# One decoder layer on one core: wider matmuls in the up stage and the projections, a first norm from transposed x, re-placed mixers and a split tail

## The chip, the cores and the metric

One core of a Trainium2 chip runs the kernel. The metric is the time of one launch in device microseconds: the median of three runs, and beside it one execution under the hardware profiler, whose trace is read here. TensorE is PE in the profile (PEld is its weight loads), VectorE is DVE, ScalarE is ACT, GpSimd is POOL, and SyncE (SP) issues most of the transfers. Each engine works through its own list in order.

## The reference

One layer, 256 tokens, 1024 channels, all in fp32. Three mixers share one projection: pooling over windows of 2 to 16, an mLSTM with 4 heads in two chunks of 128 tokens, and causal attention with 8 heads of 64 (one block of 256 keys, so plain causal softmax here).

```python
h = rmsnorm(x, ln1_g[l])
z = h @ w_in[l]                      # 1024 -> pool | mq mk | mv | mo | mi mf | aq ak av
...
mix = jnp.concatenate([po, hm, ao], axis=-1)
x = x + mix @ w_out[l]               # 1024 -> 1024
h2 = rmsnorm(x, ln2_g[l])
u = causal_dwconv(h2 @ w_up[l], ffn_conv[l])          # 1024 -> 2*2816, 3 taps
x = x + (jax.nn.silu(u[..., :D_FF]) * u[..., D_FF:]) @ w_down[l]   # 2816 -> 1024
```

## The kernel before, in words

All weights are read once, as 48 units of about 1 MB (`raw`, four buffers): 11 for the projection (`IN_UNITS`: of, vi, pool, mq, mk, and akA to avB for the two groups A and B of attention heads), 4 for W_out, 22 for W_up (a unit is a pair of 128 gate and 128 value columns), 11 for W_down. Each fp32 product is made of three matmuls in fp32r, a rounded fp32: a unit is split into `hi`, rounded on ACT (`split_hi`), and `lo` = raw − hi on DVE (`split_lo`), and so is the activation (`h_hi`, `h_lo`, later `mix_hi`, `a_hi` and so on); the matmuls are hi·hi, hi·lo and lo·hi, summed in PSUM. The last `split_lo` of a unit issues the load of the unit four further.

The stages follow one another: `of` and `vi` (gates, values), the other projections with the mixers between them, W_out with the residual (`xs` holds x by rows), the second norm, the first two up pairs by rows (`up_rows`, tile `upr`, transposed afterwards), the 20 other up pairs by columns (weights stationary, 256 tokens streaming), then the down stage into four PSUM blocks `acc[t, c]` (two halves of tokens, two of columns).

In the up stage PE works on pair i while ACT and DVE finish pair i−1: the last tap is a scaled copy on ACT (`fy`), the two others are DVE operations on `fy` that read PSUM, then silu on ACT, a product on DVE, and the split into `a_hi` (ACT) and `a_lo` (DVE). Between these lie the two halves of the next unit's split.

Everything ahead of the first up pair is cut into pieces, entered by `put(key, function, what it needs)`, and issued in the order of the numbers in the table `PLACE`; a piece without one has its number from `at`. `need` sets what a projection piece waits for. The order in the table is thus the order on every engine.

Names that come back below: `pg`, the transposes of the gates on PE, which need the evictions of of and vi and so the first norm's factors (`n1r`); `far` and `mb`, which carry a running maximum of the gates to DRAM and back to all partitions; `mqT` and `mkT`, the four-tap convolution of mLSTM's q and k (three DVE operations a tile, after `mqz`, `mkz`); `aqAsq`, squares of a projected query that ACT reads from PSUM.

Of the kernel before, what the change touches and what calls it, by code (L numbers as in the profile page):

```python
# [118 lines left out]
def kernel(  # L119
# [55 lines left out]
    def split_lo(u, part, parts):  # L175
        if u not in lo_t:
            lo_t[u] = wpool.tile([P, UMAX], F32R, tag="lo", name=f"lo{u}", bufs=HL_BUFS)
        n = unit_cols(u)
# [1 line left out]
        nc.vector.tensor_sub(lo_t[u][:, s], raw_t[u][:, s], hi_t[u][:, s].bitcast(F32))  # L180
# [24 lines left out]
    def load_part(u, c, parts):  # L205
        n = UMAX // parts
        nc.sync.dma_start(raw_t[u][:, c * n:(c + 1) * n], wg[u][:, c * n:(c + 1) * n])

    for q in range(4):
        c = slice(KT * (q > 0) + 2 * S * q, KT + 2 * S * (q + 1))  # L210
# [1 line left out]
        load_part(0, q, 4)
    for t in range(NT):
        load_part(1, t, 2)
        nc.sync.dma_start(xs[:, t], x[t * P:(t + 1) * P])
# [1005 lines left out]
```

## The time and the profile before

| what | value |
|---|---|
| median of three runs | 314.95 us (314.52 to 315.57) |
| the profiled execution | 314.13 us |
| its span, first to last instruction | 312.4 us |
| granted clock of TensorE, mean | 0.998 |
| busy: PE, DVE, ACT, POOL | 299.7, 227.3, 184.7, 11.9 us |
| read from HBM | 53.86 MB |
| up stage | 132.4 to 247.7 us |
| down stage's matmuls | 247.7 to 308.6 us |

Busy shares are averages over the stages; what a stage is worth is read from the engine that bounds it there. A row of waits names the waiting engine, its tile and line, what ended the wait, the sum, the number of times and the longest. A row of the chain gives start, length and what ran. A row of groups gives line, engine, operation, output and inputs with their shapes, the count, then busy time, mean ns of one, and the idle time ahead of them.

### The profile page before, as it was taken

Reading aid. Unit: us, or ns where it says so; the run is one execution under the profiler, and the core shown is the slowest. Engines: PE = TensorE matmul, PEld = TensorE weight load, DVE = VectorE, ACT = ScalarE, POOL = GpSimd, SP = SyncE. Lnnn points to the kernel's source line nnn. Section 1 sums busy time; section 2 is a strip of 40 time slices with the busy share of each in tenths; the row PEclk is TensorE's granted clock in tenths of the full one; section 3 lists DMA queues with packets and bytes.
Section 4 is the critical chain, followed back from the end, with each engine's and each line's share of the span. In section 5 each row is a group of like instructions: output and inputs, shape, how many; then the busy total and the mean of one; then the engine's idle time right before and its main releaser. Section 6 shows DMA issues by size and latency. Waiting matters only on the chain.

```text
span 312.4 us, 5418 instructions
## 1 busy us (share of the span) xinstructions
PE 299.7 (96%) x2132; PEld 274.4 (88%) x2132; DVE 227.3 (73%) x444; ACT 184.7 (59%) x359; POOL 11.9 (4%) x30
## 2 busy tenths in 40 slices
PE   7987969899999999999999999999999999999995
PEld 3877969899987789999999999999999988888883
DVE  2756899999869667689988788788788786534111
ACT  3884659977878526858566475565664594324000
POOL 1004540000000000000000000000000000000000
PEclk9999999999999999999999999999999999999999
DMA  7997616333514760151564463554644649600003
GB/s 232 426 410 325 221 66 259 134 136 134 212 60 137 269 266 2 56 217 58 214 237 168 150 250 141 193 213 137 212 193 148 231 159 403 270 2 0 0 12 125
DMA packets 9545, 55.26 MB, mean 177 GB/s; under 512 B 1060, under 2 KB 1328, under 8 KB 3632
## 3 DMA queue, kind: packets, MB, share of 16 engines
q1 hardware_dynamic: 9216, 53.99, 46.7%
q10 hardware_dynamic: 304, 0.92, 0.8%
q8 instruction: 17, 0.28, 0.4%
q14 instruction: 8, 0.07, 0.1%
HBM read 53.86 MB, written 1.05 MB: 176 GB/s over the span
## 4 chain that ended last, share of the span: by engine, by line
PE 80%; DMA 7%; ACT 6%; DVE 5%; issue 1%; SPq 0%; ACTq 0%; DVEq 0%
PE dn L818 19%; PE up L306 12%; PE up L304 12%; PE up L305 12%; PE wo L818 7%; DMA xs<-in_x 2%; ACT hi L173 2%; DVE lo L180 2%; DMA raw<-in_wg 2%; DMA raw<-in_w 2%; PE upr L313 1%; DVE mqT L470 1%; PE upr L315 1%; PE upr L314 1%; DMA far<-mr 1%; PE akB L313 1%
## 5 line engine op out<-in xcount | busy, mean ns | idle before, releaser
L180 DVE TENSOR_TENSOR lo<-raw,hi 128x1024 fp32r<-128x1024 f32 (+2 forms) x102 | 116.1, 1160 | 25.6 <-ACT hi L173 25.5
L173 ACT ACTIVATE hi<-raw 128x1024 fp32r<-128x1024 f32 (+2 forms) x102 | 98.2, 992 | 27.5 <-PE dn L818 18.6
L304 PE MATMUL up<-h_hi,hi 128*128 128x256 f32 x320 | 90.3, 282 | 0.0
L306 PE MATMUL up<-h_hi,lo 128*128 128x256 f32 x320 | 90.2, 282 | 0.0
L305 PE MATMUL up<-h_lo,hi 128*128 128x256 f32 x320 | 90.1, 281 | 0.0
L304 PEld LDWEIGHTS up<-h_hi,hi 128*128 128x128 f32 x320 | 60.7, 190 | 0.0
L306 PEld LDWEIGHTS up<-h_hi,lo 128*128 128x128 f32 x320 | 60.6, 189 | 0.0
L305 PEld LDWEIGHTS up<-h_lo,hi 128*128 128x128 f32 x320 | 60.6, 189 | 0.0
L1075 DVE SCALAR_TENSOR_TENSOR fy<-up,par,fy 128x255 f32<-128x255 f32 x88 | 41.8, 480 | 15.1 <-ACT fy L1072 13.5
L1072 ACT ACTIVATE fy<-up,par 128x256 f32<-128x256 f32 x44 | 20.1, 466 | 32.0 <-PE up L306 32.0
L818 PE MATMUL dn<-hi,a_lo 128*128 128x512 f32 x88 | 28.1, 393 | 0.0
L818 PE MATMUL dn<-lo,a_hi 128*128 128x512 f32 x88 | 28.1, 393 | 0.0
L818 PE MATMUL dn<-hi,a_hi 128*128 128x512 f32 x88 | 28.1, 392 | 0.0
L818 PEld LDWEIGHTS dn<-hi,a_lo 128*128 128x128 f32 x88 | 16.5, 188 | 3.8
L818 PEld LDWEIGHTS dn<-lo,a_hi 128*128 128x128 f32 x88 | 16.5, 188 | 3.8
L818 PEld LDWEIGHTS dn<-hi,a_hi 128*128 128x128 f32 x88 | 16.4, 188 | 3.7
L231 ACT ACTIVATE a_hi<-fy 128x256 fp32r<-128x256 f32 x22 | 9.2, 418 | 11.8 <-DVE fy L1081 11.8
L1123 DVE TENSOR_TENSOR xs<-dn,xs 128x512 f32<-128x512 f32 (+1 forms) x5 | 2.7, 579 | 16.7 <-PE dn L818 16.7
L818 PE MATMUL wo<-hi,mix_hi 128*128 128x512 f32 x32 | 11.2, 412 | 0.0
L818 PE MATMUL wo<-lo,mix_hi 128*128 128x512 f32 x32 | 10.6, 393 | 0.0
L818 PE MATMUL wo<-hi,mix_lo 128*128 128x512 f32 x32 | 10.6, 392 | 0.0
L1080 ACT ACTIVATE fy<-fy 128x256 f32<-128x256 f32 x22 | 9.0, 408 | 2.2 <-DVE fy L1075 2.2
(286 smaller groups left out, 521.3 us busy)
## 6 DMA issues: line engine op xcount, KB each, us to landing
raw<-in_w SPq DMA_DIRECT2D x46, 1024.0 KB, 4.8
raw<-in_wg SPq DMA_DIRECT2D x4, 260.0 KB, 5.3
raw<-in_wg SPq DMA_DIRECT2D x2, 520.0 KB, 6.8
xs<-in_x SPq DMA_DIRECT2D x2, 512.0 KB, 7.8
x_t<-in_xt SPq DMA_DIRECT2D x3, 256.0 KB, 5.1
mb<-far ACTq DMA_DIRECT2D x1, 768.0 KB, 3.8
out_y<-xs SPq DMA_DIRECT2D x3, 256.0 KB, 2.0
par<-in_params SPq DMA_DIRECT2D x1, 337.0 KB, 9.8
```

The lines of the kernel that those rows point to most:

```text
L173: nc.scalar.activation(hi_t[u][:, s], raw_t[u][:, s], AF.Copy)
L180: nc.vector.tensor_sub(lo_t[u][:, s], raw_t[u][:, s], hi_t[u][:, s].bitcast(F32))
L231: nc.scalar.activation(hi, src, AF.Copy)
L304: nc.tensor.matmul(dst, a, h_hi[:, k, :], start=k == 0, stop=False)
L305: nc.tensor.matmul(dst, a, h_lo[:, k, :], start=False, stop=False)
L306: nc.tensor.matmul(dst, b, h_hi[:, k, :], start=False, stop=k == KT - 1)
L313: nc.tensor.matmul(dst, h_hi[:, k, ts_], hw[:, k, :], start=k == 0, stop=False)
L314: nc.tensor.matmul(dst, h_hi[:, k, ts_], lw[:, k, :], start=False, stop=False)
L818: nc.tensor.matmul(acc[t, c], a, b[:, k, o:o + n], start=st and i == 0, stop=sp and i == 2)
L1072: nc.scalar.activation(y, ps[j], AF.Copy, scale=pcol(c0 + 4 * NPAIR))
L1075: nc.vector.scalar_tensor_tensor(y[:, d:], ps[j][:, :S - d], pcol(c0 + 2 * NPAIR * tap), y[:, d:], op0=ALU.mult, op1=ALU.add)
L1080: nc.scalar.activation(y_t[i, 0], y_t[i, 0], AF.Silu)
```

## The change

Six things change together.

1. Up pairs 2 to 21: `h_hi` and `h_lo` become halves of one tile `h_2`, and w_hi multiplies both in one matmul of 512 columns; w_lo multiplies h_hi alone, 256. A unit is 16 matmuls of 512 and 16 of 256, where it was 48 of 256. The two halves of the result are added afterwards: a copy `zl` on ACT, an add `z` on DVE, both of 512 columns; the taps read `z` in SBUF and alternate between the two tiles. PSUM for it is a new pool of two two-bank tiles, in the place of the mixers' one.
2. The attention's projections are made in pairs (key and query of a group, both values): a unit holds half the rows for both, and a matmul has 512 columns (144 of them for 288). The first two up pairs do the same (48 for 96). The units' order is now of, vi, mq, mk, A0, A1, pool, B0, B1, V0, V1.
3. The first norm's sums are taken from the transposed x: four squares on ACT, three adds on DVE, four one-column matmuls (`n1s`). `xs` is loaded after unit 3 instead of ahead of unit 2. All eight row blocks of `of` are plain fp32 matmuls (16, where 8 were, with 24 in fp32r).
4. The transfers of `far` and `mb` are issued by SP instead of ACT.
5. `PLACE` is new throughout, and the second norm's pieces are cut finer (three transposes to a PSUM bank).
6. The last output block (token half 1, column half 1) is added to `xs` after unit 8; the rest of it runs as 12 matmuls of 384 and 12 of 128 columns with their own adds and transfers.

```diff
-    "rbt": 7.327, "rb": 9.568, ("of", 0): 6.2, ("of", 1): 6.6, ("vi", 0): 7.109, ("vi", 1): 7.926, "setup":
...
+    ("f", 0): 2.300, ("of", 0, 0): 2.350, ("of", 1, 0): 2.400, ("f", 1): 2.450, ("sq", 0): 2.500, ("h", 0): 2.550,
...
-IN_UNITS = ["of", "vi", "pool", "mq", "mk", "akA", "aqA", "akB", "aqB", "avA", "avB"]
+IN_UNITS = ["of", "vi", "mq", "mk", "A0", "A1", "pool", "B0", "B1", "V0", "V1"]
+PAIRS = {"A": ("akA", "aqA"), "B": ("akB", "aqB"), "V": ("avA", "avB")}
...
+    h_2 = cpool.tile([P, KT, 2, S], F32R, name="h_2")
+    h_hi, h_lo = h_2[:, :, 0, :], h_2[:, :, 1, :]
...
+    def next_loads():
+        load(RAW_BUFS - 1)
+        for t in range(NT):
+            nc.sync.dma_start(xs[:, t], x[t * P:(t + 1) * P])
+        load(RAW_BUFS)
...
+    def first_square(p):
+        ks = slice(*PARTS[p])
+        nc.scalar.activation(sqk[:, ks, :], xk[:, ks, :], AF.Square)
+
+    def first_sums_t():
+        ps = aux([P, NT], "n1s")
+        for t in range(NT):
+            for k in range(2):
+                nc.tensor.matmul(ps[:, t:t + 1], sqk[:, k, t * P:(t + 1) * P], ones[:, :1], start=k == 0,
+                                 stop=k == 1)
...
+        for k in (2 * half, 2 * half + 1):
+            kk = k if first else k + 4
+            nc.tensor.matmul(dst, h_hi[:, kk, ts_], hw[:, k, :], start=kk == 0, stop=False)
+            nc.tensor.matmul(dst, h_hi[:, kk, ts_], lw[:, k, :], start=False, stop=False)
+            nc.tensor.matmul(dst, h_lo[:, kk, ts_], hw[:, k, :], start=False, stop=kk == KT - 1)
...
-        nc.scalar.dma_start(sb["far"].rearrange("b h c -> h b c"), sb["mr"].rearrange("h (b c) -> h b c", c=P))
+        nc.sync.dma_start(sb["far"].rearrange("b h c -> h b c"), sb["mr"].rearrange("h (b c) -> h b c", c=P))
...
-        nc.scalar.dma_start(mb, sb["far"].partition_broadcast(P))
+        nc.sync.dma_start(mb, sb["far"].partition_broadcast(P))
...
+            for k in range(KT):
+                a, b = (w[:, k, j * P:j * P + P] for w in (hw, lw))
+                nc.tensor.matmul(ps[:, j], a, h_2[:, k].rearrange("p c t -> p (c t)"), start=k == 0, stop=False)
+                nc.tensor.matmul(ps[:, j, :S], b, h_hi[:, k, :], start=False, stop=k == KT - 1)
+
+    def up_sum(i):
+        ps = up_t[i]
+        zl = big(f"zl{i}")[:, :2 * S].rearrange("p (j t) -> p j t", t=S)
+        nc.scalar.activation(zl, ps[:, :, S:], AF.Copy)
+        z = big(f"z{i}")[:, :2 * S].rearrange("p (j t) -> p j t", t=S)
+        nc.vector.tensor_add(z, ps[:, :, :S], zl)
+        up_t[i] = [z[:, j, :] for j in range(2)]
...
+    finish(1, 1, queue=None)
...
+    for h, (sub, queue) in enumerate((((0, 384), nc.scalar), ((384, 512), nc.sync))):
+        acc[1, 1] = psum_u.tile([P, 2, 2 * S], F32, tag="up", name=f"tail{h}", bufs=2)[:, 0]
+        for i in last:
+            down(i, 1, (1,), last, sub)
+        finish(1, 1, sub, queue)
```

The re-placing shows best on DVE, where the first unit of attention is split. Before, unit 5 (akA; `lo5` is its second half here) on DVE:

```order
L457 TENSOR_TENSOR mqz1_496<-mq1_425,rb_114 128x256
L470 SCALAR_TENSOR_TENSOR mqT0_444<-mqz0_441,par_77,mqT0_444 128x255
L470 SCALAR_TENSOR_TENSOR mqT0_444<-mqz0_441,par_77,mqT0_444 128x254
L470 SCALAR_TENSOR_TENSOR mqT0_444<-mqz0_441,par_77,mqT0_444 128x253
L470 SCALAR_TENSOR_TENSOR mqT1_513<-mqz1_496,par_77,mqT1_513 128x255
L470 SCALAR_TENSOR_TENSOR mqT1_513<-mqz1_496,par_77,mqT1_513 128x254
L470 SCALAR_TENSOR_TENSOR mqT1_513<-mqz1_496,par_77,mqT1_513 128x253
L457 TENSOR_TENSOR mkz0_535<-mk0_482,rb_114 128x256
L180 TENSOR_TENSOR lo5_423<-raw5_211,hi5_421 128x1024
L180 TENSOR_TENSOR lo6_480<-raw6_286,hi6_478 128x1024
```

After the change the same place on DVE, where the first attention unit is unit 4 (A0) and the second unit 5 (A1):

```order
L503 TENSOR_TENSOR mqz0_375<-mq0_270,rb_114 128x256
L190 TENSOR_TENSOR lo4_377<-raw4_181,hi4_373 128x1024
L661 COPY cols_125<-mcols_391 128x2x4
L190 TENSOR_TENSOR lo5_414<-raw5_208,hi5_369 128x1024
L190 TENSOR_TENSOR lo4_377<-raw4_181,hi4_373 128x1024
L516 SCALAR_TENSOR_TENSOR mqT0_429<-mqz0_375,par_80,mqT0_429 128x255
L516 SCALAR_TENSOR_TENSOR mqT0_429<-mqz0_375,par_80,mqT0_429 128x254
L516 SCALAR_TENSOR_TENSOR mqT0_429<-mqz0_375,par_80,mqT0_429 128x253
L190 TENSOR_TENSOR lo6_453<-raw6_266,hi6_412 128x1024
L190 TENSOR_TENSOR lo5_414<-raw5_208,hi5_369 128x1024
```

The six taps and mkz stood between akA's split and what came ahead; now both halves of A0's split stand ahead of the first tap, and three taps ahead of the end of A1's. On PE, `pg` followed directly on vi and n1r; it now stands 12 matmuls of mq behind vi.

The gates' maximum before, on ACT (`hi3` is the unit of mq, `hi4` of mk):

```order
L597 DMA far_348<-mr_327 4x3x128
L600 DMA mb_118<-far_348 128x1536
L173 ACTIVATE hi3_333<-raw3_170 128x1024
L173 ACTIVATE hi4_390<-raw4_172 128x1024 x2
L173 ACTIVATE hi5_421<-raw5_211 128x1024 x2
```

And after the change on SP, among the loads (`raw7` is B0, `raw8` B1, `raw10` V1):

```order
L176 DMA raw6_266<-in_w 128x2048
L643 DMA far_334<-mr_328 4x3x128
L176 DMA raw7_350<-in_w 128x2048
L646 DMA mb_119<-far_334 128x1536
L176 DMA raw8_448<-in_w 128x2048
L176 DMA raw10_455<-in_w 128x2048
```

Both transfers left ACT, where splits stood behind them, for SP, where one load stands between them and the others behind.

One unit of the up stage on DVE, before (pair 11; `lo28` is the split of the unit that PE needs next):

```order
L1075 SCALAR_TENSOR_TENSOR fy110_2451<-up110_2331,par_77,fy110_2451 128x255
L1075 SCALAR_TENSOR_TENSOR fy110_2451<-up110_2331,par_77,fy110_2451 128x254
L1075 SCALAR_TENSOR_TENSOR fy111_2455<-up111_2332,par_77,fy111_2455 128x255
L1075 SCALAR_TENSOR_TENSOR fy111_2455<-up111_2332,par_77,fy111_2455 128x254
L180 TENSOR_TENSOR lo28_2461<-raw28_2187,hi28_2459 128x1024
L1081 TENSOR_TENSOR fy111_2455<-fy110_2451,fy111_2455 128x256
L180 TENSOR_TENSOR lo28_2461<-raw28_2187,hi28_2459 128x1024
L232 TENSOR_TENSOR a_lo_1684<-fy111_2455,a_hi_1683 128x256
```

and the same pair on DVE after the change:

```order
L1143 TENSOR_TENSOR z11_2092<-up11_2000,zl11_2090 128x512
L190 TENSOR_TENSOR lo28_2053<-raw28_1874,hi28_2037 128x1024
L1156 SCALAR_TENSOR_TENSOR fy110_2096<-z11_2092,par_80,fy110_2096 128x255
L1156 SCALAR_TENSOR_TENSOR fy111_2098<-z11_2092,par_80,fy111_2098 128x255
L1156 SCALAR_TENSOR_TENSOR fy110_2096<-z11_2092,par_80,fy110_2096 128x254
L1156 SCALAR_TENSOR_TENSOR fy111_2098<-z11_2092,par_80,fy111_2098 128x254
L1162 TENSOR_TENSOR fy111_2098<-fy110_2096,fy111_2098 128x256
L190 TENSOR_TENSOR lo29_2110<-raw29_1931,hi29_2094 128x1024
L239 TENSOR_TENSOR a_lo_1466<-fy111_2098,a_hi_1465 128x256
```

The add `z` is new at the unit's start, the taps alternate between the two tiles, and the halves of the split have moved half a unit ahead: the first half of unit 29 stands where the second of unit 28 stood.

More of the change, by code (lines that the diff above doesn't have):

```diff
@@ L29 @@
 WARM = 8
-FULL = (0, 1)
+PARTS = ((0, 2), (2, 4), (4, 6), (6, 8))
+FULL = range(4)
 HL_BUFS = 4
@@ L137 @@
     mix = ExitStack()
+    psum_m = mix.enter_context(tc.tile_pool(name="psum_m", bufs=4, space=bass.MemoryType.PSUM))
     mpool = mix.enter_context(tc.tile_pool(name="mpool", bufs=1))
@@ L203, with load_part @@
     raw_t[1] = wpool.tile([P, UMAX], F32, tag="raw", name="raw1", bufs=RAW_BUFS)
[L205 to L210, printed above, removed]
+    def load_part(u, a, b):
+        c = slice(a * UMAX // KT, b * UMAX // KT)
+        nc.sync.dma_start(raw_t[u][:, c], wg[u][:, c])
+    for a, b in PARTS:
+        c = slice(KT * (a > 0) + S * a, KT + S * b)
         nc.sync.dma_start(x_t[:, c], xt[:, c])
[L212 to L215, printed above, removed]
+        load_part(0, a, b)
+    for a in (0, 4):
+        load_part(1, a, a + 4)
     load(2)
@@ L333, with first_full, first_hi @@
     h_f = h_fb[:, :KT * S].rearrange("p (k c) -> p k c", c=S)
-    sq1 = wpool.tile([P, UMAX], F32, tag="lo", name="sq1", bufs=HL_BUFS)
+    sq1 = wpool.tile([P, UMAX], F32, tag="lo", name="sq1", bufs=HL_BUFS)[:, :KT * S]
+    sqk = sq1.rearrange("p (k c) -> p k c", c=S)
     rb = cpool.tile([P, S], F32, name="rb")
-    def pair(q):
-        return slice(2 * q, 2 * q + 2)
-    def first_full(q):
-        for k in (2 * q, 2 * q + 1):
+    def first_full(p):
+        for k in range(*PARTS[p]):
             nc.vector.tensor_scalar(h_f[:, k, :], xk[:, k, :], g1[:, k:k + 1], None, op0=ALU.mult)
-    def first_hi(q):
-        if q in FULL:
-            nc.scalar.activation(h_hi[:, pair(q), :], h_f[:, pair(q), :], AF.Copy)
+    def first_hi(p):
+        ks = slice(*PARTS[p])
+        if p in FULL:
+            nc.scalar.activation(h_hi[:, ks, :], h_f[:, ks, :], AF.Copy)
@@ L347, in first_hi, with first_lo @@
         else:
-            for k in (2 * q, 2 * q + 1):
+            for k in range(*PARTS[p]):
                 nc.scalar.activation(h_hi[:, k, :], xk[:, k, :], AF.Copy, scale=g1[:, k:k + 1])
-    def first_lo(q):
-        if q in FULL:
-            nc.vector.tensor_sub(h_lo[:, pair(q), :], h_f[:, pair(q), :], h_hi[:, pair(q), :].bitcast(F32))
+    def first_lo(p):
+        ks = slice(*PARTS[p])
+        if p in FULL:
+            nc.vector.tensor_sub(h_lo[:, ks, :], h_f[:, ks, :], h_hi[:, ks, :].bitcast(F32))
@@ L354, in first_lo @@
         else:
-            for k in (2 * q, 2 * q + 1):
+            for k in range(*PARTS[p]):
                 nc.vector.scalar_tensor_tensor(h_lo[:, k, :], xk[:, k, :], g1[:, k:k + 1],
                                                h_hi[:, k, :].bitcast(F32), op0=ALU.mult, op1=ALU.subtract)
-    n1v = []
-    def first_sum(t):
-        if not n1v:
-            n1v.append(tpool.tile([P, NT], F32, tag="n1v", name="n1v"))
-        nc.vector.tensor_scalar(n1v[0][:, t:t + 1], sst[t], 1.0 / D, EPS, op0=ALU.mult, op1=ALU.add)
+    def next_loads():
[3 more added lines that the diff above has]
+        load(RAW_BUFS)
@@ L366, in first_factors, with first_mean @@
+    def first_mean():
+        nc.vector.tensor_scalar(n1v, r_t["s"], 1.0 / D, EPS, op0=ALU.mult, op1=ALU.add)
     def first_factors():
@@ L424, in bulk_rows, with bulk_pair @@
         product_rows(u, ps_t[name, t], t, range(4 * half, 4 * half + 4))
+    def bulk_pair(name, t, half):
+        u, first = U[name], name[1] == "0"
+        if first and half == 0:
+            pr = mm([P, 512], f"{name[0]}{t}")
+            for c, n in enumerate(PAIRS[name[0]]):
+                ps_t[n, t] = pr[:, 256 * c:256 * c + 256]
+            ps_t[name[0], t] = pr
+        dst, ts_ = ps_t[name[0], t], slice(t * P, (t + 1) * P)
+        hw, lw = (d[u][:, :2048].rearrange("p (k c) -> p k c", c=512) for d in (hi_t, lo_t))
+        for k in (2 * half, 2 * half + 1):
[3 more added lines that the diff above has]
+            nc.tensor.matmul(dst, h_lo[:, kk, ts_], hw[:, k, :], start=False, stop=kk == KT - 1)
     def bulk_cols(name, j, half):
@@ L816, in rows_product @@
                 for c in cs:
-                    o, n = chunks[c]
-                    nc.tensor.matmul(acc[t, c], a, b[:, k, o:o + n], start=st and i == 0, stop=sp and i == 2)
+                    o, n = 512 * c + sub[0], sub[1] - sub[0]
+                    nc.tensor.matmul(acc[t, c][:, :n], a, b[:, k, o:o + n], start=st and i == 0, stop=sp and i == 2)
     def w_out(i, t, k, cs=(0, 1)):
@@ L849 @@
         put(("lo", 1, q), do(split_lo, 1, q, 4), ("hi", 1, q), at=(0.5, 1, 4.45, 4.55)[q])
-    for t in range(NT):
-        put(("n2", t), do(norm_square, t, 0, 1, "n1", sq1[:, t * D:(t + 1) * D]), at=(4.3, 4.6)[t])
-        put(("sum", t), do(first_sum, t), ("n2", t), at=4.65)
+    for p in range(NP):
+        put(("sq", p), do(first_square, p), at=2 * p - 8.45)
+    put("ld", next_loads, ("of", 1, NP - 1), *((n, p) for n in ("h", "l", "sq") for p in range(NP)), at=0.5)
+    for n in range(3):
+        put(("sa", n), do(first_add, n), *((("sq", 2 * n), ("sq", 2 * n + 1)) if n < 2 else (("sa", 0), ("sa", 1))),
+            at=(-5.5, -1.2, -1)[n])
+    put("n1s", first_sums_t, ("sa", 2), at=4.55)
+    put("sum", first_mean, "n1s", at=4.65)
     n = 4
-    done = {}
+    done, part = {}, {}
     for name in IN_UNITS[1:]:
-        f = bulk_rows if name[:2] in ("vi", "av", "aq", "ak") else bulk_cols
+        two = name[0] in PAIRS
+        f = bulk_pair if two else bulk_rows if name == "vi" else bulk_cols
         order = [(0, 0), (0, 1), (1, 0), (1, 1)]
-        for j, half in sorted(order, key=lambda o: o[::-1]) if name == "vi" else order:
+        for j, half in sorted(order, key=lambda o: o[::-1]) if two or name == "vi" else order:
             put(("b", n), do(f, name, j, half), at=n)
-            done[name, j] = ("b", n)
+            for m in PAIRS[name[0]] if two else (name,):
+                done[m, j] = ("b", n)
+            part[n] = (n // 4, half)
             n += 1
@@ L924 @@
     for t in range(NT):
-        put(("mN", t), do(mnum_t, t), *(("me", h) for h in range(4)), ("vi", 0), ("vi", 1))
+        put(("mN", t), do(mnum_t, t), *(("me", h) for h in range(4)), ("vi", 0), ("vi", 1), "setup")
         put(("md", t), do(mnum, t), ("mN", t), "gce")
@@ L987 @@
         if n < 8:
-            half = n // 6
-            need(("b", n), ("lo", 1, 1 + 2 * half), ("l", 1 + 2 * half))
+            half = part[n][1]
+            need(("b", n), *(("lo", 1, q) for q in range(2 * half, 2 * half + 2)),
+                 *(("l", p) for p in range(NP) if PARTS[p][0] < 4 * half + 4))
         elif n < 44:
-            need(("b", n), ("lo", n // 4, n % 2), ("l", 3))
+            need(("b", n), ("lo", *part[n]))
         elif n < 56:
@@ L1110 @@
-    split(U_DOWN + 1, 1)
-    def down(i, t, cs=(0, 1)):
+        for m in (0, 1) if i == 2 else (i - 1,):
+            if m > 1:
+                up_sum(m)
+            if i < NPAIR and m:
+                split_hi(u + 2, 0, 2)
+            up_last(m)
+            if i < NPAIR and m:
+                split_hi(u + 2, 1, 2)
+            if m > 1:
+                split_lo(u + 1, 1, 2)
+            up_taps(m)
+            up_gate(m)
+            if i < NPAIR and m:
+                split_lo(u + 2, 0, 2)
+            up_out(m)
@@ L1113, in down @@
+    def down(i, t, cs=(0, 1), span=(0, N_DOWN - 1), sub=(0, 512)):
         if i == 0:
             for c in cs:
-                acc[t, c] = (mm if t == 1 and c else aux)([P, 512], f"dn{t}{c}")
-        rows_product(U_DOWN + i, (a_hi, a_lo), 2 * i, i == 0, i == N_DOWN - 1, t, cs)
-    def finish(t, c, parts=1):
-        n = 512 // parts
-        for i in range(parts):
-            s = slice(c * 512 + i * n, c * 512 + i * n + n)
-            nc.vector.tensor_add(xs[:, t, s], acc[t, c][:, i * n:i * n + n], xs[:, t, s])
-            (nc.scalar if i else nc.sync).dma_start(out[t * P:(t + 1) * P, s], xs[:, t, s])
@@ L1126, with finish @@
-    for i in range(N_DOWN - 2):
-        for t in range(NT):
-            down(i, t)
-            split(U_DOWN + i + 2, t)
-    last = (N_DOWN - 2, N_DOWN - 1)
+                acc[t, c] = aux([P, 512], f"dn{t}{c}")
+        rows_product(U_DOWN + i, (a_hi, a_lo), 2 * i, i == span[0], i == span[1], t, cs, sub=sub)
+    def finish(t, c, sub=(0, 512), queue=nc.sync):
+        s = slice(c * 512 + sub[0], c * 512 + sub[1])
+        nc.vector.tensor_add(xs[:, t, s], acc[t, c][:, :sub[1] - sub[0]], xs[:, t, s])
+        if queue is not None:
+            queue.dma_start(out[t * P:(t + 1) * P, s], xs[:, t, s])
@@ L1131 @@
+    last = (N_DOWN - 2, N_DOWN - 1)
+    for i in range(last[0]):
+        down(i, 0)
+        split(U_DOWN + i + 2, 0)
+        down(i, 1, (0,))
+        down(i, 1, (1,), (0, last[0] - 1))
+        split(U_DOWN + i + 2, 1)
+    finish(1, 1, queue=None)
     for i in last:
@@ L1134 @@
         finish(0, c)
-    for c in range(2):
+    for i in last:
+        down(i, 1, (0,))
+    finish(1, 0)
+    for h, (sub, queue) in enumerate((((0, 384), nc.scalar), ((384, 512), nc.sync))):
+        acc[1, 1] = psum_u.tile([P, 2, 2 * S], F32, tag="up", name=f"tail{h}", bufs=2)[:, 0]
         for i in last:
-            down(i, 1, (c,))
-        finish(1, c, 1 + c)
+            down(i, 1, (1,), last, sub)
+        finish(1, 1, sub, queue)
 def _units(w_in, w_out, w_up, w_down):
```

190 lines of the change are left out of this document (99 added, 91 removed), and 97 rows, old and new, of the table PLACE.

## The prediction

> **What bounds the kernel now.** I read the page first (busy shares, the slices, the chain by engine), then busy time by stage, then what TensorE (PE) waited for, then the chain in order of time.
>
> ```profile
> PE 299.7 (96%) x2132; PEld 274.4 (88%) x2132; DVE 227.3 (73%) x444; ACT 184.7 (59%) x359; POOL 11.9 (4%) x30
> ...
> PE   7987969899999999999999999999999999999995
> ...
> PE 80%; DMA 7%; ACT 6%; DVE 5%; issue 1%; SPq 0%; ACTq 0%; DVEq 0%
> ```
>
> PE is busy 96% of the span and is 80% of the chain; its idle tenths lie in the first eight slices. By stage (projections' first part, mixers and W_out, up, down; the columns are the stretch, its length, then PE, PEld, DVE, ACT, POOL):
>
> ```profile
> 8.00:64.00 56.00, 49.05 (x402) 46.32 (x400) 45.39 (x89) 42.34 (x82) 10.37 (x19) 1.00 0.66 255
> 64.00:132.40 68.40, 68.39 (x485) 60.58 (x482) 52.54 (x153) 48.23 (x125) 0.00 (x0) 1.00 0.39 143
> 132.40:247.70 115.30, 115.30 (x970) 115.14 (x969) 99.51 (x170) 70.60 (x127) 0.00 (x0) 1.00 0.50 182
> 247.70:308.60 60.90, 60.87 (x264) 49.19 (x263) 27.04 (x27) 20.85 (x23) 0.00 (x0) 1.00 0.35 132
> ```
>
> So from 64 us on PE never waits, and only cheaper matmuls help there. PE's clock is full throughout (1.00). The 56 us before hold 6.95 us of PE idle, and PE's waits name it:
>
> ```profile
> PE akA L314 <- DVE lo L180: 2.4, 1, 2.4
> PE pg L571 <- ACT gates L451: 1.4, 2, 1.1
> PE mq L306 <- DVE lo L180: 1.2, 1, 1.2
> ...
> PE akB L313 <- ACT aqAsq L509: 0.8, 1, 0.8
> PE mq L304 <- ACT hi L173: 0.7, 1, 0.7
> PE of L314 <- DVE lo L180: 0.3, 1, 0.3
> ```
>
> They sum to 6.8 us. A wait costs a little more than its row, as a restart shows:
>
> ```profile
> 42.77 0.28 PE L313 MATMUL akA<-hi,h_hi 128*128 128x256 f32 x1
> 45.44 0.39 PE L314 MATMUL akA<-lo,h_hi 128*128 128x256 f32 x1 [2.39 <-DVE lo L180]
> ```
>
> Start to start this is 2.67 us, and a step is 0.12, so the wait cost 2.55, 0.16 over its row. Seven stalls (pg has two) are thus worth 6.8 + 7×0.16 = 7.9 us.
>
> **The change, part by part.** Widths first. The steps come from the chain and the stage above:
>
> ```profile
> 117.31 0.88 PE n2pt L283 x8
> ...
> 132.46 1.02 PE up L1028 x8
> 247.68 60.91 PE dn L818 x264
> 308.61 0.42 DVE xs L1123
> ```
>
> The up stage's 960 matmuls of 256 columns take 115.30 − 1.02 = 114.28 us, 0.119 each; a 512-wide one takes 60.91/264 = 0.231. Two merged into one save 0.238 − 0.231 = 0.0074 us. The up stage has 16×20 = 320 such merges: **−2.4 us**. Projections (144) and the first two up pairs (48): **−1.4 us**. [...]
>
> The "of" unit and the first sums are dearer:
>
> ```profile
> L439 PE MATMUL of<-raw,h_f 128*128 128x260 f32 x16 | 4.0, 392 | 1.1 <-DVE h_f L342 1.1
> ...
> L378 PE MATMUL n1r<-diag,ones 128*128 128x128 f32 x4 | 0.6, 274 | 0.0
> ```
>
> The 16 records are 8 plain fp32 matmuls, 0.5 us each. Eight more cost 4.0 and replace 24×0.12 = 2.9: **+1.1**. The four new one-column sums (n1s) have no row; the two n1r matmuls cost 0.3 each, so four lie between 0 and 1.2; a single column streams less than 128, so I take **+0.4**. The squares and adds that replace the xs squares run on ACT and DVE while PE is in "of", before anyone needs them.
>
> Now the stalls, **−7.9**. The rows that make them:
>
> ```profile
> 7.09 7.78 DMA xs<-in_x
> ...
> 25.03 3.21 DMA far<-mr
> 28.26 0.36 ACTq L600
> 28.67 1.06 ACT hi L173
> 29.75 1.71 DVE lo L180
> ```
>
> ```profile
> 39.70 4.22 DVE L470 SCALAR_TENSOR_TENSOR mqT<-mqz,par,mqT 128x255 f32<-128x255 f32 x6
> 43.83 0.42 DVE L457 TENSOR_TENSOR mkz<-mk,rb 128x256 f32<-128x256 f32 x1
> 44.17 2.35 DVE L180 TENSOR_TENSOR lo<-raw,hi 128x1024 fp32r<-128x1024 f32 x2
> ```
>
> ```profile
> 8.00:24.00 16.00, 14.18 (x110) 12.97 (x109) 11.18 (x23) 14.17 (x31) 0.00 (x0) 1.00 1.03 418
> ```
>
> - akA: six taps and mkz (4.6 us) stand ahead of the split that PE wants. Now both halves of A0's lo stand ahead of the taps.
> - mq, both rows: ACT held the issue of mb (L600) until far landed, and the splits behind it were late. On SP it holds no split. Price: on SP the load of B0 stands between the two, that of B1 behind mb. A far of 3.2 us can delay only those two, whose matmuls come after A0, A1 and pool (5.7 us a unit); I cost it at nothing, at 3.2 if that cover is gone.
> - pg: 12 matmuls of mq (1.4 us) now lie between vi and pg, and the norm no longer waits for xs, which landed at 14.87. Without its 1.05 MB ahead, at 418 GB/s, the later weights land 2.5 us earlier.
> - akB: needs the banks that aqAsq still reads; the pool unit (48×0.119 = 5.7 us) now stands between. of: no split is left to wait for.
>
> What is late next? DVE: its 97.9 busy us (45.39 + 52.54) out of 124.4 become as many out of some 116, 79% to 84%. I give back a quarter, **+2.0** (ends 0 and 7.9): nearer to none, because each stall's cause is moved by name; not none, because some 200 other pieces move too.
>
> Up stage, beside PE. PE's unit becomes 16×(0.231 + 0.119) = 5.60 us, from 5.71. DVE gains the add z, ACT the copy zl:
>
> ```profile
> L180 DVE TENSOR_TENSOR lo<-raw,hi 128x1024 fp32r<-128x1024 f32 x38 | 46.4, 1220 | 0.0
> L1075 DVE SCALAR_TENSOR_TENSOR fy<-up,par,fy 128x254 f32<-128x254 f32 x43 | 20.7, 482 | 1.5
> L1075 DVE SCALAR_TENSOR_TENSOR fy<-up,par,fy 128x255 f32<-128x255 f32 x43 | 20.6, 478 | 12.7 <-ACT fy L1072 12.7
> L1081 DVE TENSOR_TENSOR fy<-fy,fy 128x256 f32<-128x256 f32 x21 | 8.8, 418 | 0.2
> L232 DVE TENSOR_TENSOR a_lo<-fy,a_hi 128x256 fp32r<-128x256 f32 x21 | 8.8, 418 | 1.0 <-ACT a_hi L231 1.0
> ...
> L828 DVE TENSOR_TENSOR xs<-wo,xs 128x512 f32<-128x512 f32 x4 | 2.6, 683 | 1.4 <-PE wo L818 1.4
> ```
>
> These five up rows sum to 105.3 us in 114 of wall clock, yet the stage shows 99.51 busy in 115.3: neighbours overlap by some 0.04 us. Per unit (115.3/5.71 = 20.2) that is 4.93 us; z adds 0.683 − 0.04: 5.57 against 5.60. That is tight. But DVE may lag: z must be read only before the unit after next takes its PSUM pair, 5.60 after its last matmul, and zl and z take some 2×0.68, so 4.2 us of lag are free. 0.2 us per unit over 20 units would still cost nothing. I take **0**. ACT has 70.60/20.2 + 0.7 = 4.2 of 5.6.
>
> Tail: 12 of 264 matmuls become 12 of 384 (between 0.119 and 0.231, so 0.175) and 12 of 128 (0.88/8 = 0.11): 12×(0.285 − 0.231) = +0.65, between 0 (columns alone count) and +1.4 (384 as dear as 512, 128 as 256). The last add shrinks from two of 256 to one of 128, and its issue no longer waits for the second: the 0.42 us row goes, −0.4 (0 to −0.4). **+0.2**.
>
> Sum: −2.4 − 1.4 + 1.1 + 0.4 − 7.9 + 2.0 + 0.2 = −8.0. The profiled execution took 314.1 us (312.4 of span, 1.7 around it), so 306.1; it lies 0.8 under the median of 314.95, so I forecast a median of **306.9**.
>
> **Rivals.** (1) The stalls come back under other names, more than half: a DVE in 45.39 of 56 us already, hi and lo re-placed among 200 pieces, two loads behind the maximum's transfers. All 7.9 back instead of 2.0 gives 312.8; half to all, 308.9 to 312.8. Against: each of the five stalls has its own moved piece. (2) DVE bounds the up stage. If neighbours don't overlap, a unit is 2×1.22 + 4×0.48 + 2×0.418 + 0.683 = 5.88, 0.28 over PE: 20×0.28 − 4.2 = 1.4, and with the wait for ACT of 12.7/20.2 = 0.63 per unit kept by half, 0.6 over, 7.8: 308 to 314.7. Against it is the overlap just shown. [...] (3) The other side, slower: the hand-overs zl, z, taps on two in-order queues don't overlap with the splits, and the copy counts in full beside the add: 5.88 + 0.68 = 6.56 per unit. 20×0.96 − 4.2 = 15 us more: 321.9. It decides from (8.0 + 4.2)/20 = 0.61 over PE's unit, 6.2 us, on. Against: ACT has 1.4 us to spare per unit and its splits stand between the hand-overs. (4) Nothing comes back and the earlier loads help: 304.9, with free sums (n1s, tail) 304.
>
> **How the numbers follow.** A median differs from no change from about 0.3% (0.9 us) on. Chances: forecast, 304.9 to 308.9: 0.55; (4) 0.10; (1) 0.19; (2) 0.10; (3) 0.05; something unseen 0.01. The range leaves out (3), the upper part of (2) (0.04) and the ends of (1) and (4) (0.05), 0.15 in all: 303.5 to 312.5. Faster holds the forecast, (4), nearly all of (1), four fifths of (2): 0.91; same 0.03; slower 0.06.
>
> **What would show it.** Right: the up stage lasts near 112 us with PE busy throughout, DVE busy near 5.4 to 5.6 us per unit; akA's, pg's and mq's waits vanish from PE's list and new ones sum to 2 or so; the stage starts near 125 to 126. Wrong: PE waits on z (DVE) or on lo in the up stage; PE's first 64 us again hold 5 us or more of idle; the load of B0 or B1 late behind far; a 512-wide step over 0.238.

## The result, and the profile after

The changed kernel takes 306.16 us in the median of four runs (304.70 to 306.95), against 314.91 before: a ratio of 0.9715, 95% interval 0.9673 to 0.9756. The forecast was 306.9, range 303.5 to 312.5. The profiled execution has a span of 304.7 us, where before it was 312.4. From the page:

```profile
PE 299.0 (98%) x1632; PEld 252.1 (83%) x1632; DVE 235.7 (77%) x467; ACT 196.6 (65%) x373; POOL 10.7 (4%) x30
...
PE   7999999999999999999999999999999999999995
...
PE 90%; DVE 4%; ACT 2%; DMA 1%; issue 1%; SPq 0%; ACTq 0%; DVEq 0%
```

The idle tenths of PE in the first eight slices are gone. What it waited for is now this, whole (waits of PE):

```profile
PE of L485 <- DMA raw<-in_wg: 1.3, 1, 1.3
PE warm L333 <- PEq L1308: 0.8, 1, 0.8
PE akAT L596 <- DVE knA L587: 0.5, 1, 0.5
```

All the stalls that the prediction named have vanished; one small one is new, ahead of the transposes of the normalised keys (`akAT`), which wait for DVE. PE still waits ahead of `of`, as it did before (1.1 us). By stage (from the first vi matmul to the first up matmul, up stage, down stage; columns as before):

```profile
15.60:126.60 111.00, 110.50 (x662) 92.92 (x662) 91.61 (x231) 83.08 (x191) 9.28 (x21) 1.00 0.50 188
126.60:239.90 113.30, 113.30 (x650) 99.04 (x649) 106.70 (x187) 85.45 (x147) 0.00 (x0) 1.00 0.53 190
239.90:301.60 61.70, 61.70 (x278) 50.73 (x276) 29.09 (x33) 20.10 (x23) 0.00 (x0) 1.00 0.34 124
```

Between the same points the kernel before shows:

```profile
12.90:132.30 119.40, 112.88 (x854) 103.04 (x853) 93.33 (x233) 86.16 (x199) 10.37 (x19) 1.00 0.49 184
132.30:247.50 115.20, 115.20 (x970) 115.04 (x969) 99.61 (x170) 70.70 (x127) 0.00 (x0) 1.00 0.51 182
247.50:308.60 61.10, 61.07 (x266) 49.39 (x264) 27.04 (x27) 20.85 (x23) 0.00 (x0) 1.00 0.35 132
```

| stretch | before | after | difference |
|---|---|---|---|
| start of the span to the first `of` matmul | 5.2 | 5.7 | +0.5 |
| `of` and the norm's sums | 7.7 | 9.8 | +2.1 |
| first vi to first up matmul | 119.4 | 111.0 | −8.3 |
| up stage | 115.2 | 113.3 | −1.9 |
| down stage's matmuls | 61.1 | 61.7 | +0.7 |
| last matmul to the end | 3.8 | 3.1 | −0.8 |
| span | 312.4 | 304.7 | −7.7 |

The differences are taken before rounding.

Most of the gain lies between the first vi matmul and the up stage, −8.3, and some of it is lost ahead of that, +2.6. The rows of that loss (before, then after, groups of PE up to 16 us):

```profile
L439 PE MATMUL of<-raw,h_f 128*128 128x260 f32 x16 | 4.0, 392 | 1.1 <-DVE h_f L342 1.1
```

```profile
L485 PE MATMUL of<-raw,h_f 128*128 128x260 f32 x32 | 9.2, 456 | 1.3 <-DMA raw<-in_wg 1.3
...
L390 PE MATMUL n1s<-ones,sq 128*128 128x1 f32 x8 | 0.9, 240 | 0.0
```

Twice the records (two to a matmul) take 9.2 us and not 8.0. The same matmuls run at two speeds, as the count of records per stretch shows (after):

```profile
5.70:9.40 3.70, 3.66 (x9) 2.92 (x10) 3.00 (x8) 2.96 (x6) 0.00 (x0) 1.00 1.03 364
9.40:14.00 4.60, 4.60 (x22) 4.00 (x21) 4.37 (x9) 2.91 (x6) 0.00 (x0) 1.00 1.01 418
```

9 records in 3.70 us, 0.41 each, then 22 in 4.60, 0.21 each; from start to start the steps are 0.433 and 0.219 us. PE ran at half rate until 9.7 us. The 1.00 in the column of the granted clock is no reading there: the trace's clock records, of which the column is an average, begin only at 9.67 us, with the grant of the full clock, and time ahead of the first record counts as 1.00. In the kernel before, the first record begins at 3.68 us.

### The profile page after: what moved, and what is told of

Its sections match the earlier page's. It is cut to its first block, busy times and chain, and to the rows that moved or that the text cites. A ratio compares the mean times of both kernels' runs of the same rounds, so it can differ in the third digit from the quotient of the medians.

```text
span 304.7 us, 4434 instructions
## 1 busy us (share of the span) xinstructions
PE 299.0 (98%) x1632; PEld 252.1 (83%) x1632; DVE 235.7 (77%) x467; ACT 196.6 (65%) x373; POOL 10.7 (4%) x30
## 4 chain that ended last, share of the span: by engine, by line
PE 90%; DVE 4%; ACT 2%; DMA 1%; issue 1%; SPq 0%; ACTq 0%; DVEq 0%
PE up L1135 24%; PE dn L862 19%; PE up L1136 12%; PE wo L862 7%; PE of L485 3%; DMA raw<-in_wg 1%; PE V L468 1%; PE upr L1081 1%; PE V L470 1%; PE upr L1082 1%; PE upr L1080 1%; PE V L469 1%; PE B L468 1%; PE tail L862 1%; PE B L470 1%; PE B L469 1%
## 5 line engine op out<-in xcount | busy, mean ns | idle before, releaser
L1135 PE MATMUL up<-h,hi 128*128 128x512 f32 x320 | 112.6, 396 | 0.0
L1136 PE MATMUL up<-h,lo 128*128 128x256 f32 x320 | 90.1, 282 | 0.0
L1135 PEld LDWEIGHTS up<-h,hi 128*128 128x128 f32 x320 | 60.1, 188 | 14.2 <-DVE z L1143 0.2
L1136 PEld LDWEIGHTS up<-h,lo 128*128 128x128 f32 x320 | 60.2, 188 | 0.0
L1156 DVE SCALAR_TENSOR_TENSOR fy<-z,par,fy 128x255 f32<-128x255 f32 (+1 forms) x80 | 33.2, 476 | 0.0
L1149 ACT ACTIVATE fy<-z,par 128x256 f32<-128x256 f32 x40 | 18.2, 503 | 4.2 <-DVE z L1143 4.2
L1143 DVE TENSOR_TENSOR z<-up,zl 128x512 f32<-128x512 f32 x20 | 13.7, 684 | 0.4 <-ACT zl L1141 0.4
L1200 DVE TENSOR_TENSOR xs<-dn,xs 128x512 f32<-128x512 f32 x4 | 2.7, 688 | 14.0 <-PE dn L862 14.0
L1141 ACT ACTIVATE zl<-up 128x512 f32<-128x512 f32 x20 | 11.7, 585 | 1.7 <-PE up L1136 1.5
L1162 DVE TENSOR_TENSOR fy<-fy,fy 128x256 f32<-128x256 f32 x22 | 9.4, 425 | 3.6 <-ACT fy L1161 2.0
```

The costliest lines, as they stand in the source:

```text
L1135: nc.tensor.matmul(ps[:, j], a, h_2[:, k].rearrange("p c t -> p (c t)"), start=k == 0, stop=False)
L1136: nc.tensor.matmul(ps[:, j, :S], b, h_hi[:, k, :], start=False, stop=k == KT - 1)
L1141: nc.scalar.activation(zl, ps[:, :, S:], AF.Copy)
L1143: nc.vector.tensor_add(z, ps[:, :, :S], zl)
L1149: nc.scalar.activation(y_t[i, j], up_t[i][j], AF.Copy, scale=pcol(Q_FC + i + NPAIR * j + 4 * NPAIR))
L1156: nc.vector.scalar_tensor_tensor(y[:, d:], up_t[i][j][:, :S - d], pcol(Q_FC + i + NPAIR * j + 2 * NPAIR * tap), y[:, d:], op0=ALU.mult, op ...
```

## The experiments

Twelve kernels. The first four start from the changed kernel itself; the others, but for the kernel before with more warm-up, start from the changed kernel with 11 warm-up matmuls. Each has its own ratio to the kernel before, timed beside it.

**More warm-up** (warm11, before_w). `WARM = 8` became `WARM = 11`, first in the changed kernel:

> The changed kernel with 11 instead of 8 warm-up matmuls, so that PE has no pause ahead of the of unit. In the changed kernel's profile the of records step by 0.433 us until 9.3 us and by 0.219 from 9.7 on, before the change by 0.219 from 5.5 on. Theory (PE was still at half rate because of the pause, and this is in the time): the step of 0.219 comes at 8 us or earlier, the of unit takes 7.0 to 8.0 us instead of 9.2, median 304.5 to 305.6, runs closer together than 304.7 to 306.95. Rival (the step is set by something else, the weights' landing): step and median stay, 306.2.

304.95 us (304.91 to 305.06), ratio 0.9702, 0.9688 to 0.9717.

```profile
L485 PE MATMUL of<-raw,h_f 128*128 128x260 f32 x32 | 7.8, 406 | 0.0
```

`of` takes 7.8 us instead of 9.2, PE's pause ahead of it is gone, and the four runs lie within 0.15 us instead of 2.25 (0.2 to 1.8 us in the later kernels with 11 warm-ups that have no longer stall). In the trace the theory holds: the half rate at the start was in the time. In the ratio it does not stand clear, since the intervals overlap. Then in the kernel before:

> The kernel before, with 11 instead of 8 warm-up matmuls. The of unit of the kernel before took 7.70 us in its profile, with PE at the full rate from the start. Theory (the rate of PE at the start is drawn anew in each run, for both kernels, and before the change it costs less, since only 8 fp32 matmuls follow): median 0.2 to 0.6 us below the kernel before, 314.1 to 314.5. Rival (the kernel before never starts at half rate): no difference at all, 314.5.

314.48 against 314.68, ratio 0.9998, 0.9983 to 1.0012. The 0.2 us less is the edge of what the theory gave and lies inside the interval, so this run does not part the two. In the changed kernel the slow start costs about 1.2 us of the median; for the kernel before, both profiles have the full clock early (3.68 and 3.51 us), and more is not shown.

The clock records of all profiles say when the grant comes: at 9.67 us in the changed kernel and 9.34 in narrow_proj below, whose `of` takes 9.2 and 9.3 us, and between 3.5 and 6.8 us in the twelve others, with 8 warm-ups (3.90 in dve_256, 5.06 in narrow_up) as with 11 (3.51 to 6.80). It differs between executions by itself. In the two late ones it had not come when PE paused between its warm-up and `of` (at 4.4 us, for 1.33 and 0.82 us); in dve_256 it came before a pause of 1.2 us, and `of` took the full 7.3. So the pause's length alone does not decide it. In the nine profiles with 11 warm-ups the pause was 0.0 to 0.8 us and the grant came by 6.80 us; why it came when it did in one execution is not shown.

**The up stage narrow again** (narrow_up).

```diff
-                nc.tensor.matmul(ps[:, j], a, h_2[:, k].rearrange("p c t -> p (c t)"), start=k == 0, stop=False)
-                nc.tensor.matmul(ps[:, j, :S], b, h_hi[:, k, :], start=False, stop=k == KT - 1)
+                nc.tensor.matmul(ps[:, j, :S], a, h_hi[:, k, :], start=k == 0, stop=False)
+                nc.tensor.matmul(ps[:, j, :S], a, h_lo[:, k, :], start=False, stop=False)
+                nc.tensor.matmul(ps[:, j, :S], b, h_hi[:, k, :], start=False, stop=k == KT - 1)
...
     def up_sum(i):
-        ...
+        up_t[i] = [up_t[i][:, j, :S] for j in range(2)]
```

> The changed kernel with its 20 up pairs back at 48 matmuls of 256 columns each (no zl, no z; the taps read PSUM), all else as changed. Theory (widths): 320 merges are undone at 0.0074 us, so the stretch from the first up matmul to the first down matmul grows from 113.4 to 115.8 us and the median from 306.2 to 308.5. Rival (the add and the copy give it back: DVE is busy 105.76 of 111.86 us in the changed up stage): the stretch stays within 0.5 us of 113.4 and the median at 306 or below.

310.68 us, ratio 0.9873 (0.9843 to 0.9904). The stage grew from 113.3 to 117.5 us, 4.2 and not 2.4. PE's waits and DVE's timeline say where the rest is:

```profile
PE up L1135 <- ACT fy L1157: 1.9, 1, 1.9
```

```profile
137.50 1.65 DVE L1152 SCALAR_TENSOR_TENSOR fy<-up,par,fy 128x255 f32<-128x255 f32 x4
```

The third unit takes the first one's PSUM pair. With z that pair is free after one add; without it only after the four taps, which end at 139.15 us; PE resumes at 139.29. (The row names ACT's silu, L1157, as what came last, but silu reads and writes SBUF only; it is the taps that read the pair.) 4.2 − 1.9 − 0.16 = 2.1 us are width, near the 2.4 of the sum. The rival, that z costs the gain, is refuted.

**One more DVE operation per up unit** (dve_256).

```diff
         nc.vector.tensor_add(z, ps[:, :, :S], zl)
+        spare = mid(f"spare{i}")
+        nc.vector.tensor_add(spare[:, :256], zl[:, 0, :256], zl[:, 1, :256])
```

> The changed kernel with one more DVE add of 256 columns per up unit (its result is not used), right behind z. DVE's unit is 5.36 us from z to z in the changed kernel's trace, PE's 5.60. Theory of the prediction (4.2 us of lag are free): the unit becomes 5.70, 0.10 over PE's, 2 us in all, which the lag hides: median 306.2, no waits of PE on z. Rival (the lag is spent when the stage starts: z of the first unit starts only at 138.0, some 5 us behind its matmuls): DVE can no longer catch up, PE waits for z in nearly every unit, some 0.10 x 18 = 1.9 us: median 308.

306.86 us, ratio 0.9771 (0.9755 to 0.9787). The median seems to speak for the prediction's account, but its profile has `of` at 7.3 us, 1.9 less than the profile of the changed kernel; against warm11, whose start is near the full rate too, it is 1.9 us more, which is what the rival gave. The up stage is longer: 114.65 us against 113.27, and 62.3 against 61.7 in the down stage. How far z lies behind PE decides. First the changed kernel: z's first and last start (a tile's row), the start of PE's second unit, the start of the down stage, and z on DVE in two units:

```profile
L1143 DVE TENSOR_TENSOR z<-up,zl x20: 681/683/693, 138.0 to 240.7; 128x512 f32<-128x512 f32 x20
```

```profile
133.06 0.39 PE L1135 MATMUL up<-h,hi 128*128 128x512 f32 x1
...
239.90 0.40 PE L862 MATMUL dn<-hi,a_hi 128*128 128x512 f32 x1
```

```profile
202.57 0.68 DVE L1143 TENSOR_TENSOR z<-up,zl 128x512 f32<-128x512 f32 x1
...
207.93 0.68 DVE L1143 TENSOR_TENSOR z<-up,zl 128x512 f32<-128x512 f32 x1
```

The first z starts 4.9 us behind the end of its matmuls, the last 0.8: DVE's unit is 207.93 − 202.57 = 5.36 us here, less than PE's, and it catches up some 0.2 us in each ((4.9 − 0.8)/19). Then with the spare add:

```profile
L1143 DVE TENSOR_TENSOR z<-up,zl x20: 681/684/687, 136.3 to 244.5; 128x512 f32<-128x512 f32 x20
```

```profile
131.33 0.39 PE L1135 MATMUL up<-h,hi 128*128 128x512 f32 x1
...
239.55 0.63 PE L862 MATMUL dn<-hi,a_hi 128*128 128x512 f32 x2
```

Here z starts 5.0 us behind at both ends. DVE's unit is 5.70 us and PE's has stretched to it, in stalls of 0.1 us that make no row among the waits. The rival holds: z ends 5.0 + 0.68 us behind the unit, where PE wants its PSUM pair again after 5.60; the lag is used up when the stage begins.

**The projections narrow again** (narrow_proj). Each 512-wide matmul of the pairs and of the first two up pairs became two of 256:

```diff
-            nc.tensor.matmul(dst, h_hi[:, kk, ts_], hw[:, k, :], start=kk == 0, stop=False)
...
+            for c in (slice(0, 256), slice(256, 512)):
+                nc.tensor.matmul(dst[:, c], h_hi[:, kk, ts_], hw[:, k, c], start=kk == 0 and c.start == 0, stop=False)
...
```

> The changed kernel with the paired projections and the first two up pairs at twice as many matmuls of 256 columns (288 and 96), same units, same order. Theory (widths): 192 merges undone at 0.0074 us, from the first vi matmul to the first up matmul 110.9 becomes 112.3 us, median 307.6. Rival (PE has waits in this stretch that take it up, or the pairs' gain is in the order and not in the width): median within 0.5 us of 306.2.

306.53 us, ratio 0.9752 (0.9735 to 0.9770). The median can't tell the two apart; the stretch from vi to up can: 112.0 us against 111.05 (changed kernel) and 111.35 (with 11 warm-ups), 0.6 to 0.9 more and not 1.4. Here the wait ahead of `akAT` hides a part:

```profile
PE akAT L597 <- DVE knA L588: 0.3, 1, 0.3
```

With the wide projections that wait is 0.5 us (changed kernel), 0.9 (warm11), 1.1 (dve_256), 1.4 (narrow_up) and 1.7 (the plain tail below), and the stretch 111.05 to 112.3; less the wait, the stretch is about 110.5 us in all five. In narrow_proj it is 111.7 less the wait. So the width is worth some 1.1 us, not far from the theory's 1.4, and the wait takes up a part of it, as the rival said.

**A0's split behind the taps** (a0_late_w), by three numbers of the table:

```diff
-("lo", 4, 1): 17.429, ("ct", "mq", 0): 17.571, ("ct", "mq", 1): 20.167
+("lo", 4, 1): 17.950, ("ct", "mq", 0): 17.400, ("ct", "mq", 1): 17.920
```

> The changed kernel with 11 warm-up matmuls (305.0 us, step of the of records even from run to run), and on DVE the second half of A0's lo placed behind the six taps of mqT, as akA's stood before the change. Theory (the order of this split took away the largest stall): by the changed kernel's trace the split moves from 32.9 to some 38.4 us while PE wants it near 36.6, so PE waits for lo some 3 us ahead of A0's second half and the median is 307.5 to 308. Rival (other pieces wait elsewhere, and the 3 us are made good by waits that vanish later): within 0.7 us of 305.0.

312.2 us, ratio 0.9926 (0.9903 to 0.9949): 7 us lost, not 3. PE's waits, and its stretches around the first of them:

```profile
PE A L469 <- DVE lo L190: 3.1, 1, 3.1
PE akAT L596 <- DVE knA L587: 1.7, 1, 1.7
PE warm L333 <- PEq L1308: 0.8, 1, 0.8
PE mS L679 <- DVE mkT L532: 0.8, 1, 0.8
```

```profile
35.20:39.00 3.80, 0.71 (x4) 0.33 (x3) 3.73 (x5) 1.82 (x4) 0.93 (x1) 1.00 0.01 2
39.00:43.20 4.20, 4.20 (x14) 3.28 (x13) 3.87 (x7) 0.51 (x1) 0.00 (x0) 0.62 0.79 298
```

The wait for lo is there at 3.1 us as expected. Two things come on top: DVE's later pieces are late too (0.8, and 0.8 more at akAT than with 11 warm-ups alone), and after the stall PE's granted clock is 0.62 for 4.2 us, which costs an estimated 1.6 us (0.38 of 4.2). (The trace has a record of half clock from 39.99 to 43.40 us.) That makes the profiled execution, 311.4 us, 6.3 longer than warm11's. The theory holds, with a price that it did not have.

**pg directly behind vi** (pg_early_w; `("vi", 0)`, `("vi", 1)` and `"pg"` at 7.80, 7.85 and 7.90):

> The changed kernel with 11 warm-up matmuls, and pg directly behind vi instead of 12 matmuls of mq later. Theory (those 12 matmuls covered the gates' eviction): PE waits for gates 0.8 to 1.5 us in two parts, median 305.8 to 306.5. Rival (the first norm from transposed x is known early enough, and the 12 matmuls cover nothing): no wait, 305.0.

305.44 us, ratio 0.9710 (0.9680 to 0.9740). PE has no wait on the gates. The rival holds: the 12 matmuls cover nothing. That leaves the earlier norm as the likely cause (ACT's `n1r`, which the gates need, starts at 14.6 us in warm11, at 16.5 before); no run takes the sums from `xs` again, so it is not shown by itself.

**far and mb issued by ACT again** (far_act_w; `nc.sync` back to `nc.scalar` in the two lines):

> The changed kernel with 11 warm-up matmuls, and far and mb issued by ACT again. Theory of the prediction (mb's issue on ACT holds the splits behind it until far has landed): ACT is held some 2 to 3 us near 27 to 30 us, the splits of A1 and pool are late, PE waits 1 to 2.2 us, median 306 to 307. Rival (the new order has the splits that are wanted next ahead of it): ACT waits, PE does not, 305.0.

305.79 us, ratio 0.9721 (0.9694 to 0.9748), 0.2% above that of warm11; the two intervals overlap, and PE's list has one short wait that warm11's has not (0.3 us, `mk` on a split by DVE). ACT's timeline:

```profile
25.24 0.51 ACTq L643 DMA_DIRECT2D far<-mr  x1
...
30.00 0.36 ACTq L646 DMA_DIRECT2D mb<-far  x1
30.06 2.00 ACT L183 ACTIVATE hi<-raw 128x1024 fp32r<-128x1024 f32 x2
```

In the new order mb is issued 4.8 us behind far, where it was 3.2, and the splits that PE wants next stand ahead of it; no row of ACT's waits names far. The rival holds within what can be told: the queue's change is worth one short wait in the profile. What removed the two waits of `mq` is then the new order and the earlier loads, which no run here takes apart.

**xs loaded ahead of unit 2 again** (xs_early_w; the two loads moved back between vi's halves):

> The changed kernel with 11 warm-up matmuls, and xs loaded between the halves of vi as before the change. Theory of the prediction (1.05 MB less ahead of the weights brings all later ones 2.5 us earlier, and this counts): vi's second half and mq land 1.2 to 2.5 us later and PE waits for their splits, median 306 to 307.5. Rival (the weights land with more than that to spare, since of's fp32 matmuls and n1s hold PE until 14 us): 305.0 to 305.3.

306.06 us, ratio 0.9725 (0.9692 to 0.9757). PE's wait, and its clock behind it:

```profile
PE mk L317 <- DVE lo L190: 1.4, 1, 1.4
```

```profile
27.70:33.00 5.30, 3.86 (x25) 3.51 (x24) 5.00 (x9) 3.76 (x5) 0.00 (x0) 0.83 0.50 182
33.00:40.00 7.00, 7.00 (x37) 6.21 (x36) 6.58 (x9) 6.11 (x10) 1.58 (x1) 0.89 0.85 295
```

mk's split is 1.4 us late, and the clock is down again behind it (0.83, 0.89; a record of half clock from 31.17 to 34.58 us). From vi to up it is 114.2 us against 111.35. ACT's first split of mq starts at 17.31 us, after a wait for its load, where it started at 14.90 in warm11 without one: the loads are late by 2.4 us or more. The theory holds in the trace, for mk and not for mq. The profiled execution (307.36) is the slowest of the four, the others (305.6 to 306.3) have a mean clock of 0.999 and 1.0, and the median's interval does not part it from warm11.

**The second half of `of` in fp32r again** (of_fp32r_w; `FULL = range(2)`, with the splits at 2.82 to 3.18 in the table):

> The changed kernel with 11 warm-up matmuls, and the second half of the of unit in three fp32r matmuls each again (24 for 8 fp32 ones, with their splits). Theory of the prediction (fp32 costs 0.5 us a matmul, 4.0 against 2.9): the of unit with n1s shrinks by 1.1 us, from 7.9 to 8.5 to some 7 us, median 304. Rival (at full rate an fp32 matmul steps by 0.44, 3.5 against 2.9 in all, and the two splits come back as a wait of PE of 0.3 to 0.5): within 0.3 us of 305.

306.55 us, ratio 0.9743 (0.9722 to 0.9764): slower. PE's waits:

```profile
PE of L323 <- ACT h L358: 1.4, 2, 1.1
...
PE of L325 <- DVE h L366: 0.5, 1, 0.5
```

Neither account foresaw the size: the splits of `h`, the activation, are not ready when PE is, 1.9 us. In this placement two of ACT's squares for the new sums stand ahead of them (8.90 to 10.03 us), so that the run shows plain matmuls to be the faster way in this order; whether another order would have the splits in time is not shown.

**The tail in one piece again** (plain_tail_w; 264 matmuls of 512, the add in two halves):

> The changed kernel with 11 warm-up matmuls, and the tail as before the change (264 matmuls of 512, the last block's add in two halves). Theory of the prediction (+0.65 for the narrow matmuls, -0.4 for the shorter end, +0.2 in all): 0.2 us faster, 304.8. By the changed kernel's trace (61.73 + 3.07 us from the first down matmul to the end, against 61.05 + 3.83 before): 0.1 slower, 305.1. Either is within what can be told; the two parts are read from the trace: 61.05 and 3.8.

305.09 us, ratio 0.9698 (0.9678 to 0.9718). The down stage's matmuls take 61.0 us and the end 3.8, against 61.7 and 3.0 with the split tail. It gains as much as it costs.

**An attempt at the last wait** (best; `("plz", 0)` from 25.167 to 26.750, `("gg", 1)` from 24.889 to 26.760, both on DVE behind knA):

> The changed kernel with 11 warm-up matmuls, and two DVE operations (the pool's first product with the norm's factors and the second gate gain, 0.33 us each) moved behind the normalised keys knA, for which PE waits 0.5 to 1.4 us ahead of akAT. Theory (DVE's order makes this last wait): the wait shrinks by 0.67 us to 0.2 to 0.3, median 304.3. Rival (knA's chain waits for ACT's squares and not for DVE's queue): the wait and 305.0 stay.

308.84 us, ratio 0.9814 (0.9789 to 0.9839): 4 us slower. The profiled execution is one of 307.13 us at a mean clock of 0.999; the three slowest of the five (308.84 to 309.44) have 0.992 and 0.993, so a part of the 4 us is a lower clock that this trace does not show. PE's waits, ACT's timeline and the chain:

```profile
PE aqAT L596 <- ACT aqA L573: 2.2, 1, 2.2
PE B L468 <- DVE knA L587: 0.8, 1, 0.8
```

```profile
55.74 0.47 ACT L573 ACTIVATE aqA<-A,n1r 128x256 f32<-128x256 f32 x1 [5.33 <-POOL pld L833]
```

```profile
51.74 0.34 DVE plz L821
...
53.00 1.47 POOL plz L828
54.52 0.40 POOL plz L830
54.91 0.07 issue
54.98 0.73 POOL pld L833
55.74 0.48 ACT aqA L573
```

plz starts a chain on POOL; ACT's aqA waits for a step of that chain, since it takes over a buffer that the chain reads (`mid`, seven buffers for all these tiles). The moved piece was off PE's path, yet it set when a buffer came free. knA is indeed earlier (it ends at 51.7 us, in warm11 at 53.9), and the wait ahead of akAT is gone; two others took its place, for knA ahead of B and for aqA.

## Why the prediction was right, point by point

The time, the sign and the place were right: 306.16 for 306.9. Its steps were right to different degrees, and that the number came so near is partly luck, as the sum at the end shows.

- *The stalls, −7.9 with 2.0 given back.* The stretch from vi to up shrank by 8.3 us; less some 1.1 for widths, 7.2 are stalls. The stall in `of` lies ahead of this stretch; without it (0.46) the sum had −7.4 and +2.0. Only one wait of 0.5 us came back (0.3 to 1.7 in the other kernels: by and large the longer, the earlier PE starts). a0_late_w shows one cause at work: the order of a single split. That DVE, busier by share, would give back a quarter is the term that was most off, by more than 1 us.
- *The causes, one by one.* akA: right; the same split late in the new order (a0_late_w) costs 7 us, of which the wait itself is 3.1. pg: the vanished wait was foreseen, but of its two reasons the 12 matmuls do nothing, which leaves the earlier norm. mq and the queue: the waits vanished, but not because SP issues the transfers; in the new order ACT issues them at hardly any price. The earlier weights by 2.5 us were right (2.4 or more in xs_early_w), and count for mk. akB: the wait vanished; that the pool unit's place did it is not shown.
- *`of` and n1s, +1.1 and +0.4.* Mis-sized, in two parts that differ in sign. At full rate (narrow_up, dve_256, xs_early_w) `of` and n1s take 7.9 us from the first `of` to the first vi matmul, against 7.7: +0.2 instead of the net 1.0 that the sum had. A plain fp32 matmul steps by 0.44 us there (7.1 us for 16; the row's 4.0 us for 8 held 0.3 us of longer steps and the modelled end of the last record), and n1s costs 0.8 and not 0.4. But the profiled execution began at half rate and lost 1.9 us. In the profile of before the full clock came at 3.68 us, so nothing there showed that start.
- *Widths, −2.4 and −1.4.* 2.1 by narrow_up and 1.1 by narrow_proj, less PE's wait. The step of 0.0074 us per merge was right for the up stage and nearly so for the projections, where a wait takes up a part.
- *The up stage at 0 for DVE.* The number was right and the reason wrong. DVE's unit is 5.36 us and not 5.57: the alternating taps take 1.66 us for four (a row of four in the timeline). But the 4.2 us of lag that were to be free are taken when the stage starts, while DVE is at the taps of the two pairs made by rows (the last of them end at 136.0 us, the first unit's matmuls at 133.1). There a DVE unit above 5.60 us costs at once, as dve_256 shows.
- *The tail, +0.2.* +0.7 and −0.8, about nothing: plain_tail_w agrees.

So misses cancelled: the stalls gave 1.8 us more than forecast and the tail 0.3, the start of PE took 1.6 and the widths gave 0.7 less. Without the slow start (warm11) the median is 2.0 us under the forecast. The rival in which DVE bounds the up stage was wrong here, as DVE's starts lie ahead of its neighbours' ends:

```profile
206.46 1.22 DVE L190 TENSOR_TENSOR lo<-raw,hi 128x1024 fp32r<-128x1024 f32 x1
207.59 0.42 DVE L239 TENSOR_TENSOR a_lo<-fy,a_hi 128x256 fp32r<-128x256 f32 x1
```

1.13 us from start to start, with a duration of 1.22.

The version that does best is the changed kernel with 11 warm-up matmuls: 304.95 us, ratio 0.9702. Its interval overlaps that of the changed kernel (0.9715), so that it is faster rests on the runs' spread and on the row of `of`.

## What to carry to other kernels

A stall of PE has a cause by name, an instruction that stands too late in another engine's order, and moving that one was worth more here than making matmuls wider (7.2 us against some 3). Before moving another, look at what it frees: a piece off the path can hold a buffer that the path wants. A lag that an engine may have counts only if it isn't used up already; read it from how far the engine starts behind at the stage's beginning and end.
